# First block up to the solve: engines in a fixed order, key weights first, the norm factor inside the scaling, values later

## The chip, the core and the metric

The kernel runs on one core of a Trainium2 chip. The metric is the time of one execution in device microseconds (us). The core has TensorE (PE in the rows; its weight loads are PEld), VectorE (DVE), ScalarE (ACT), GpSimd (POOL) and SyncE (SP), which here only issues DMA transfers. Each engine has a queue of its own and works it off strictly in order; an instruction that waits holds up all that stands behind it on that engine.

## The reference

Two transformer blocks run one after the other on 256 tokens of width 1024, each ending in a mixture of experts. The change touches the start of the first block. There the tokens `x` and 256 context tokens `ctx` are normed and modulated with vectors that come from the conditioning input `c`:

```python
m_lat = jnp.split((s_lat @ w_mod[l] + b_mod[l])[:, None, :], 6, axis=-1)
h_lat = modulate(rmsnorm(x_lat, norm1_g[l]), m_lat[0], m_lat[1])
h_ctx = modulate(rmsnorm(x_ctx, norm1_g[l]), m_ctx[0], m_ctx[1])
mix_lat, mix_ctx = token_mixers(h_lat, h_ctx, w_in[l], ...)
```

`token_mixers` projects h with `w_in` into the inputs of four token mixers. One of them, the gated delta net, needs keys, values and queries (after a convolution of five taps and a SiLU), a decay `g` and a factor `beta`, and in every chunk the inverse of a triangular matrix:

```python
lower = jnp.where(strict, jnp.einsum('bnhid,bnhjd->bnhij', kb, kc) * decay, 0.0)
t_inv = lax.linalg.triangular_solve(eye + lower, eye, left_side=True, lower=True, unit_diagonal=True)
```

The matrix needs keys, decay and beta. Values and queries come in only when the inverse is there.

## The kernel before

All token data is kept with features on the partitions and 512 tokens (256 of `x`, 256 of `ctx`) in the free dimension. Every float32 product that matters is made of three: a weight is split into `whi` (a rounded copy, ScalarE) and `wlo` (the rest, a subtraction), the activations into `hh` and `hl`, and PE multiplies whi by hh, whi by hl and wlo by hh (`mm3`, L275). `wsplit` makes the pair for 128 output columns; a counter `nsplit` gives every `share`-th `wlo` to GpSimd and the others to VectorE.

`block1` runs in this order:

- norm: squares of x1 and xctx, their sums on PE (`san`, `ssn`), and `rs` by a logarithm and an exponential on ScalarE (L289, L290), for each half apart; x1 and xctx are multiplied by it in place (L638), and x1 is loaded again later (L658).
- `shift_scale(j)`, j from 0 to 7: loads 1 MB of `w_mod_a`, multiplies on PE (`ma`), copies (`msa`), folds on PE (`mq`), and makes shift `modT` and scale `A` of feature block j (L607, L608).
- the key loop, k from 0 to 7: `modulated(k)` makes `ht` (GpSimd, L618, for some k ScalarE), `hh` and `hl`; then come six products into the key sums `pk[0]`, `pk[1]` (`pj` in the rows) and two into `abp`, the inputs of decay and beta.
- behind it: convolution of both key halves (`conv`: a copy `raw` on ScalarE, five passes `cacc` on VectorE, a SiLU), the value projections, decay and beta, the norm of the keys (`l2`), outer products `rE` on GpSimd (L771), their sums `pE` and `brow` on PE, the key products `gram`, and from these `Lc` and its transpose `Lt` on VectorE.
- `solve()`: 31 steps on VectorE, each a product `tmp` (L837) and a sum `X` (L838), then two transposes `Y`.
- `projections()`, woven into the solve as filling: queries, gate, `nk`, `nq`, `nv`, `dv`, `dk`, `dq` and `fu`, each a weight load `win`, two splits and two times 24 products (L275) of 512 or 256 columns, and `mods`, which multiplies further parts of `w_mod` (`mp`). `totok` turns a projected value to token order by PE transposes (`tk`) and a copy by `S.evac`, which takes ScalarE and VectorE in turn.

Behind this come the mixers (`delta`, attention, Fourier), the output projection, the experts, and the second block.

What sets the order: a scheduler orders each engine's queue by the program's order and by when it takes an instruction to be ready. `keep_in_program_order` binds an instruction to its place in the program. Weights go through a ring of four slots of 1 MB that SyncE fills in program order; a load waits until its slot's last reader is done, and the loads behind it wait too.

Of the kernel before, what the change touches and what calls it, by code (L numbers as in the profile page):

```python
# [9 lines left out]
F32 = mybir.dt.float32  # L10
# [170 lines left out]

class K:
# [331 lines left out]
def block1(S):  # L514
# [43 lines left out]
    nc.scalar.activation(sc[:, :, 0:3], V("c3").rearrange("p (k i) -> p k i", i=3), AF.Silu)  # L558

# [36 lines left out]
    def shift_scale(j):  # L596
# [11 lines left out]
        nc.vector.scalar_tensor_tensor(A1[:, j, :], q[:, 2:4], bm1[:, j:j + 1], bc(V("g1")[:, j:j + 1], [128, 2]), op0=ALU.add, op1=ALU.mult)  # L608

    def modulated(k):  # L610
        for i, x in enumerate((x1, xctx)):
            t = he.tile([128, 256], F32, name="ht", bufs=3)
            q = slice(256 * i, 256 * i + 256)
            a, b = A1[:, k, i:i + 1], S.modT[:, k, i:i + 1]
            if i == 1 and k % 2:
                nc.scalar.activation(t, x[:, k, :], AF.Identity, bias=b, scale=a)
            else:
                nc.gpsimd.tensor_scalar(t, x[:, k, :], a, b, op0=ALU.mult, op1=ALU.add)  # L618
# [20 lines left out]
    for j in (1, 2):  # L639
        shift_scale(j)  # L640
# [1445 lines left out]
```

## Time and profile before

| | us |
|---|---|
| three runs | 2063.32, 2068.43, 2068.35 |
| median | 2068.35 |
| the profiled execution, time | 2067.2 |
| the profiled execution, span | 2065.4 |
| first key product (PE) | 26.66 |
| last product of the key loop (PE) | 57.28 |
| first product of the filling (PE) | 89.30 |
| last step of the solve ends (DVE) | 153.38 |
| last copy of the filling (ACT) | 202.97 |
| first load of the output projection's weights | 330.96 |

The page's first part gives PE 1651.5 us busy (80%), DVE 648.3 (31%), ACT 446.4 (22%) and POOL 207.9 (10%). The shares are means over stages with different limits: from about 350 to 1290 us the DMA engines are full with the experts' weights, while before that PE, the chains on ACT and DVE, and PE's granted clock matter. So the first 203 us are read stage by stage.

### The profile page before, as it was taken

The page shows a single profiled execution, that of the slowest core. Times are in us where ns is not written, and L with a number is a line of the kernel's source. Part 1 is how long each engine was busy: PE and PEld are TensorE (multiplying, and loading weights), DVE is VectorE, ACT ScalarE, POOL GpSimd, SP SyncE. Part 2 cuts the span into 40 slices and gives each one's busy share as a digit, 9 for nine tenths or more (in the row PEclk, how much of TensorE's full clock was granted, in tenths as well). Part 3 has the DMA queues.
Part 4 walks back from the last instruction along what each step waited for, and adds up shares of the span by engine and source line. Part 5 has one row for each costly group of instructions (what it writes and reads, how often), then busy time and mean ns, then how long its engine had stood idle before and what let it go on. Part 6 is the DMA issues. An engine that isn't in the chain of part 4 may idle for free.

```text
span 2065.4 us, 25484 instructions
## 1 busy us (share of the span) xinstructions
PE 1651.5 (80%) x10702; PEld 853.1 (41%) x10702; DVE 648.3 (31%) x1326; ACT 446.4 (22%) x794; POOL 207.9 (10%) x273
## 2 busy tenths in 40 slices
PE   6879999866666667566666666899998999999997
PEld 3656457511121112111121111788998444444443
DVE  4793683311111111001011110799655121222212
ACT  4542233300010001000010001576543111111111
POOL 2433432100000000000000000243111000000000
PEclk8999999888887887888898788999999999999998
DMA  7466457999999999999999999434548899999994
GB/s 296 144 218 228 159 203 314 416 431 430 431 431 430 431 430 430 431 431 431 430 431 431 430 430 427 162 124 153 203 182 337 353 431 430 430 430 431 431 430 195
DMA packets 61798, 723.70 MB, mean 350 GB/s; under 512 B 6944, under 2 KB 8736, under 8 KB 11120
## 3 DMA queue, kind: packets, MB, share of 16 engines
q1 hardware_dynamic: 60560, 717.95, 83.8%
q0 software_dynamic: 1120, 4.08, 0.5%
q8 instruction: 86, 1.41, 0.3%
q14 instruction: 32, 0.26, 0.0%
HBM read 720.96 MB, written 1.05 MB: 350 GB/s over the span
## 4 chain that ended last, share of the span: by engine, by line
DMA 47%; PE 38%; DVE 9%; ACT 3%; issue 2%; POOL 1%; SPq 0%; DVEq 0%; ACTq 0%; POOLq 0%
DMA w_up<-in_w_up_dram 15%; DMA w_down<-in_w_down_dram 14%; DMA w_gate<-in_w_gate_dram 13%; PE pj L275 6%; PE Yp L1852 5%; PE U L1852 4%; PE G L1852 4%; DMA w<-in_w_dram 4%; PE pw L275 2%; PE gx L1852 2%; DVE tmp L837 1%; PE ya L275 1%; PE cmb L1852 1%; PE mp L545 1%; PE yb L275 1%
## 5 line engine op out<-in xcount | busy, mean ns | idle before, releaser
L1221 PE MATMUL U<-w_up,xg 128*32 128x512 f32 x1024 | 172.8, 808 | 119.8 <-DMA w_up<-in_w_up_dram 119.8
L1221 PE MATMUL Yp<-w_down,hT 128*32 128x512 f32 x1024 | 161.5, 762 | 101.7 <-DMA w_down<-in_w_down_dram 96.2
L1221 PE MATMUL G<-w_gate,xg 128*32 128x512 f32 x1024 | 160.0, 676 | 57.8 <-DMA w_gate<-in_w_gate_dram 57.7
L1329 DVE TENSOR_TENSOR hs<-hs,U 128x512 f32<-128x512 f32 x16 | 11.0, 687 | 437.2 <-PE U L1221 437.2
L1221 PEld LDWEIGHTS U<-w_up,xg 128*32 128x32 f32 x1024 | 33.2, 129 | 259.8 <-DMA w_up<-in_w_up_dram 162.8
L275 PE MATMUL pj<-uh,whi 128*128 128x256 f32 x408 | 118.1, 290 | 3.2 <-ACT uh L1452 3.2
L1221 PEld LDWEIGHTS Yp<-w_down,hT 128*32 128x32 f32 x1024 | 31.5, 124 | 210.9 <-DMA w_down<-in_w_down_dram 140.0
L1852 PE MATMUL U<-w,xg 128*64 128x512 f32 x512 | 113.7, 594 | 6.0 <-DMA w<-in_w_dram 6.0
L275 PE MATMUL pj<-uh,wlo 128*128 128x256 f32 x408 | 116.7, 286 | 1.1 <-DVE wlo L257 1.1
L275 PE MATMUL pj<-ul,whi 128*128 128x256 f32 x408 | 115.7, 284 | 0.0
L1852 PE MATMUL Yp<-w,hT 128*64 128x512 f32 x512 | 113.8, 596 | 2.3 <-DVE ysl L1924 1.6
L1852 PE MATMUL G<-w,xg 128*64 128x512 f32 x512 | 112.6, 592 | 0.0
L1343 ACT COPY ys<-Yp 128x256 f32<-128x256 f32 x17 | 6.3, 373 | 479.0 <-DVE ys L1342 479.0
L256 ACT CAST whi<-win 128x1024 fp32r<-128x1024 f32 x72 | 75.1, 1048 | 71.4 <-PE pj L275 41.6
L1221 PEld LDWEIGHTS G<-w_gate,xg 128*32 128x32 f32 x1024 | 29.4, 115 | 145.0 <-DMA w_gate<-in_w_gate_dram 87.1
L1221 PE MATMUL cmb<-seln,ys 128*128 128x256 f32 x256 | 78.6, 422 | 13.0 <-DVE ys L1342 9.5
L1465 POOL DMA_DIRECT2D dist<-in_dist_dram x1 | 0.6, 606 | 877.0 <-DMA w_down<-in_w_down_dram 877.0
L1342 DVE COPY ys<-Yp 128x256 f32<-128x256 f32 x17 | 7.2, 424 | 244.9 <-PE Yp L1221 244.9
L1339 DVE SCALAR_TENSOR_TENSOR x<-cmb,modT,x 128x256 f32<-128x256 f32 x128 | 59.5, 483 | 77.0 <-PE cmb L1221 77.0
L275 PEld LDWEIGHTS pj<-uh,whi 128*128 128x128 f32 x408 | 77.5, 190 | 5.1 <-ACT uh L1452 3.4
L275 PEld LDWEIGHTS pj<-uh,wlo 128*128 128x128 f32 x408 | 77.5, 190 | 2.4 <-DVE wlo L257 1.5
L1221 PEld LDWEIGHTS cmb<-seln,ys 128*128 128x128 f32 x256 | 43.4, 195 | 83.3 <-DVE x L1339 37.3
(583 smaller groups left out, 2949.1 us busy)
## 6 DMA issues: line engine op xcount, KB each, us to landing
w<-in_w_dram SPq DMA_DIRECT2D x94, 2048.0 KB, 25.6
w_gate<-in_w_gate_dram SPq DMA_DIRECT2D x64, 2048.0 KB, 38.8
w_up<-in_w_up_dram SPq DMA_DIRECT2D x64, 2048.0 KB, 38.8
w_down<-in_w_down_dram SPq DMA_DIRECT2D x60, 2048.0 KB, 38.9
wmod<-in_w_mod_dram SPq DMA_DIRECT2D x40, 1024.0 KB, 4.9
win<-in_w_in_dram SPq DMA_DIRECT2D x36, 1024.0 KB, 4.9
wmod<-in_w_mod_a_dram SPq DMA_DIRECT2D x8, 1024.0 KB, 7.4
wout<-in_w_out_dram SPq DMA_DIRECT2D x8, 1024.0 KB, 6.9
```

What stands on the lines that cost most here:

```text
L256: self.nc.scalar.copy(hi, x)
L275: self.nc.tensor.matmul(out, a(k), b(k), start=(n == 0), stop=(n == 3 * K - 1))
L545: nc.tensor.matmul(out, l, r, start=a, stop=b)
L837: nc.vector.tensor_tensor(tv, X[:, 0:i, 0:i], bc(Lt[:, i, None, 0:i], [128, i, i]), op=ALU.mult)
L1221: nc.tensor.matmul(out, l, r, start=a, stop=b)
L1329: nc.vector.tensor_tensor(hs, hs, U, op=ALU.mult)
L1339: nc.vector.scalar_tensor_tensor(x1[:, k, :], pc, S.modT[:, 40 + k, 0:1], x1[:, k, :], op0=ALU.mult, op1=ALU.add)
L1342: nc.vector.tensor_copy(ys[:, 0:256], Y[:, 0:256])
L1343: nc.scalar.copy(ys[:, 256:512], Y[:, 256:512])
L1465: nc.gpsimd.dma_start(dist, I["dist"])
L1852: tc.keep_in_program_order(nc.tensor.matmul(o, l, r, start=a, stop=b))
```

## The change

- A wrapper `Engines` binds every TensorE, VectorE and ScalarE instruction from the key weights' load to the solve's input `Lt` to its place in the program. GpSimd and SyncE stay with the scheduler.
- The key weights `win` are loaded ahead of the eight `wmod` loads, and are split before the norm's logarithm.
- The norm factor: one logarithm and one exponential over both halves; `rs` enters the scaling (`ht` = x times A times rs on VectorE), ScalarE adds the shift for `hh`, VectorE makes `hl`. x1 and xctx are not written, and x1 is not loaded again.
- `shift_scale` has two halves that are placed between the key products of the step before.
- `warm` issues products whose result nobody reads: six ahead of the norm's sums and two behind each of the first two `ma`.
- The value projections and the turning of values and keys to token order move from before the solve into `projections()`.
- GpSimd loses `ht`, the outer products and, by `share` staying at 4 during the solve, most `wlo`; the copies `egl` move behind the solve's input. `totok` copies on ScalarE only.
- Behind the keys, ScalarE does exponentials first, then both SiLU and squares, both logarithms, both exponentials.

```diff
+class InOrder:
+    def __getattr__(self, name):
+        f = getattr(self.engine, name)
+        return lambda *a, **k: self.tc.keep_in_program_order(f(*a, **k))
+class Engines:
+    def __init__(self, tc):
+        self.tensor, self.vector, self.scalar = (InOrder(tc, e) for e in (tc.nc.tensor, tc.nc.vector, tc.nc.scalar))
+        self.gpsimd, self.sync = tc.nc.gpsimd, tc.nc.sync
...
+    def warm(self, pool, tag, n):
+        p = pool.tile([128, 512], F32, name="warm", tag=tag)
+        for _ in range(n):
+            self.tc.keep_in_program_order(self.tc.nc.tensor.matmul(p[:, 0:256], self.c("ones"), self.C[:, 0:256], start=True, stop=True))
...
+            nc.vector.scalar_tensor_tensor(t[:, q], x[:, k, :], A1[:, k, i:i + 1], rs[:, q], op0=ALU.mult, op1=ALU.mult)
+            nc.scalar.activation(H[0][:, k, q], t[:, q], AF.Identity, bias=S.modT[:, k, i:i + 1])
+            nc.vector.scalar_tensor_tensor(H[1][:, k, q], t[:, q], S.modT[:, k, i:i + 1], H[0][:, k, q].bitcast(F32), op0=ALU.add, op1=ALU.subtract)
...
+    nc = S.nc = Engines(tc)
+    wk = wload(0)
+    blocks = [shift_scale(j) for j in range(8)]
...
     for k in range(8):
-        if k < 5:
-            shift_scale(k + 3)
-        if k == 5:
-            wv = wload(1)
-            wvs = [S.wsplit(sb, wv, 0, tags=("Lc", "Lt"))]
-        modulated(k)
+        if k < 6:
+            next(blocks[k + 2])
+        keys(0, k)
+        if k < 7:
+            modulated(k + 1)
+        if k < 6:
+            next(blocks[k + 2])
+        keys(1, k)
...
-    wvs.append(S.wsplit(sp, wv, 1))
-    nc.gpsimd.dma_start(x1, I["xl"].rearrange("p (k t) -> p k t", k=8))
+    wv = wload(1)
+    wvs = S.wsplit(sb, wv, 0, tags=("Lc", "Lt"))
...
-        S.evac(dst[:, :, 128 * P:128 * P + 128], tp)
+        S.evac(dst[:, :, 128 * P:128 * P + 128], tp, "s")
...
-        nc.gpsimd.tensor_tensor(dst, bc(vec[:, None, :], [128, 32, vec.shape[1]]), bc(mask[:, :, None], [128, 32, vec.shape[1]]), op=ALU.mult)
+        nc.vector.tensor_tensor(dst, bc(vec[:, None, :], [128, 32, vec.shape[1]]), bc(mask[:, :, None], [128, 32, vec.shape[1]]), op=ALU.mult)
...
     def projections():
+        for P in range(2):
+            a = conv(proj(wv, P, 512, None if P else wvs), 4 + P, 512)
+            yield 5.1
+            totok(vtok, a, P)
+        for P in range(2):
+            totok(ktok, kn[:, P, :], P)
...
-    S.share = 1
     weave(solve(), fill)
```

SyncE now issues the key weights `win` behind x1 and xctx, then the small `wab` and all eight `wmod`; before, one `wmod` stood ahead of the key weights and seven behind.

ScalarE at the norm of the keys, before: `l2rk` is the norm factor of a half, by a logarithm (L289) and an exponential (L290), `eg` and `D` are exponentials for the decay.

```order
L289 ACTIVATE l2rk_561<-l2p,cst 128x512
L290 ACT_TABLE_LOAD
L290 ACTIVATE l2rk_561<-l2rk_561 128x512
L761 ACTIVATE eg<-gp 128x192
L289 ACT_TABLE_LOAD
L289 ACTIVATE l2rk_569<-l2p,cst 128x512
L290 ACT_TABLE_LOAD
L290 ACTIVATE l2rk_569<-l2rk_569 128x512
L782 ACTIVATE D<-pE 128x512 x2
```

And after, from the SiLU of the keys (`cacc`) on (in this listing every ordered instruction carries the wrapper's line, L189; `l2k` is a square, `ln` the decay's logarithm):

```order
L189 ACT_TABLE_LOAD
L189 ACTIVATE cacc<-cacc 128x512
L189 ACTIVATE l2k<-cacc 128x512
L189 ACTIVATE cacc<-cacc 128x512
L189 ACTIVATE l2k<-cacc 128x512
L189 ACT_TABLE_LOAD
L189 ACTIVATE ln<-u_481 128x32
L189 ACTIVATE l2rk<-l2p,cst 128x512 x2
L189 ACT_TABLE_LOAD
L189 ACTIVATE l2rk<-l2rk 128x512 x2
```

From the keys' SiLU to the last exponential of the key norm there are three table loads now; before, there were six (the ones at L681, L731 and L733 stand ahead of the rows shown).

VectorE at the solve's start, before (L678 and L680 are convolution passes of the queries; `t` and `Lc` build the solve's input, `Lt` is its transpose):

```order
L824 TENSOR_TENSOR Lc<-t_740,beta 128x32x16
L825 TENSOR_TENSOR t_740<-D,gm 128x512
L826 TENSOR_TENSOR Lc<-t_740,brow 128x32x16
L678 TENSOR_SCALAR cacc<-raw,vec_97 128x256
L828 STREAM_TRANSPOSE Lt<-Lc 128x32x32
L250 COPY ktok<-tk 128x4x128
L837 TENSOR_TENSOR tmp<-X,Lt 128x1
```

And after:

```order
L189 TENSOR_TENSOR Lc<-t_626,beta 128x32x16
L189 TENSOR_TENSOR t_626<-D,gm 128x512
L730 TENSOR_SCALAR cacc<-raw,vec_97 128x512
L189 TENSOR_TENSOR Lc<-t_626,brow 128x32x16
L732 SCALAR_TENSOR_TENSOR cacc<-raw,vec_97,cacc 128x512
L189 STREAM_TRANSPOSE Lt<-Lc 128x32x32
L732 SCALAR_TENSOR_TENSOR cacc<-raw,vec_97,cacc 128x512
L895 TENSOR_TENSOR tmp<-X,Lt 128x1
```

The first pass over the first value half (L730) now stands ahead of the last `Lc`.

VectorE at the solve's end, before, where `nv` is a copy by `totok` and `Y` the solve's result:

```order
L837 TENSOR_TENSOR tmp<-X,Lt 128x900
L838 TENSOR_REDUCE X<-tmp 128x30
L837 TENSOR_TENSOR tmp<-X,Lt 128x961
L838 TENSOR_REDUCE X<-tmp 128x31
L250 COPY nv<-tk 128x4x128
L842 STREAM_TRANSPOSE Y_1299<-X 128x1024
```

And after, where L274 makes the `wlo` of the two `nv` halves:

```order
L895 TENSOR_TENSOR tmp<-X,Lt 128x841
L274 TENSOR_TENSOR wlo<-win,whi 128x1024
L896 TENSOR_REDUCE X<-tmp 128x29
L274 TENSOR_TENSOR wlo<-win,whi 128x1024
L895 TENSOR_TENSOR tmp<-X,Lt 128x900
L896 TENSOR_REDUCE X<-tmp 128x30
```

The copy has left VectorE's queue, and two splits for PE's filling stand behind the product of step 29.

## Rows read from the trace of the kernel before

**Rows 1.** Busy time by stretch: us, PE, PEld, DVE, ACT, POOL, granted clock, DMA share, GB/s.
```profile
600.00:1200.00 600.00, 388.98 (x2232) 101.27 (x2236) 58.55 (x118) 30.45 (x71) 0.00 (x0) 0.81 1.01 431
```

**Rows 2.** Timeline of SP's DMA issues: start us, us, what, count.
```profile
330.96 5.53 SPq L238 DMA_DIRECT2D wout<-in_w_out_dram  x4
```

**Rows 3.** Timeline at the start: start us, us, engine, line, what [idle before, releaser].
```profile
11.67 1.06 ACT L433 ACTIVATE sqn<-xctx 128x1024 f32<-128x1024 f32 x1 [1.40 <-DMA xctx<-in_xctx_dram]
...
19.52 0.40 PE L282 MATMUL ma<-wmod,sc 128*32 128x256 f32 x1 [0.40 <-DMA wmod<-in_w_mod_a_dram]
...
21.35 1.98 ACT L256 CAST whi<-win 128x1024 fp32r<-128x1024 f32 x2
...
26.66 0.76 PE L545 MATMUL pj<-hh,whi 128*128 128x512 f32 x1 [6.07 <-DVE hh L620]
```

**Rows 4.** Busy time by stretch, columns as in Rows 1: the clock's falls and rises.
```profile
24.00:26.00 2.00, 0.00 (x0) 0.00 (x0) 2.00 (x2) 0.09 (x1) 2.00 (x1) 0.50 0.00 0
36.00:38.00 2.00, 2.00 (x19) 0.98 (x19) 0.36 (x1) 0.24 (x1) 0.00 (x0) 0.70 0.01 4
150.00:152.00 2.00, 0.00 (x0) 0.00 (x0) 1.97 (x2) 0.00 (x0) 0.00 (x0) 0.50 0.00 0
164.00:166.00 2.00, 2.00 (x13) 1.36 (x15) 0.00 (x0) 0.00 (x0) 0.00 (x0) 1.00 0.00 0
```

**Rows 5.** Timeline of PE inside the key loop, columns as in Rows 3.
```profile
40.48 0.40 PE L282 MATMUL ma<-wmod,sc 128*32 128x256 f32 x1
...
41.48 0.45 PE L545 MATMUL abp<-hh,wabs 128*64 128x512 f32 x1
...
42.23 0.50 PE L545 MATMUL mq<-cst,msa 128*128 128x2 f32 x4
...
42.59 0.48 PE L545 MATMUL pj<-hl,whi 128*128 128x512 f32 x1
```

**Rows 6.** Timeline from the key loop's end to the first filling projection.
```profile
57.73 0.58 ACT L675 COPY raw<-pj 128x512 f32<-128x512 f32 x1
...
57.92 2.39 POOL L257 TENSOR_TENSOR wlo<-win,whi 128x1024 fp32r<-128x1024 f32 x1 [1.50 <-ACT whi L256]
...
58.34 2.25 DVE L678 TENSOR_SCALAR cacc<-raw,vec 128x512 f32<-128x512 f32 x1 [0.42 <-ACT raw L675]
...
63.75 4.05 DVE L680 SCALAR_TENSOR_TENSOR cacc<-raw,vec,cacc 128x512 f32<-128x512 f32 x6
...
76.10 1.28 ACT L290 ACT_TABLE_LOAD   x1
...
86.07 2.07 PE L545 MATMUL brow<-rE,cst 128*128 128x512 f32 x2
...
88.08 1.30 PE L545 MATMUL gram<-kn 64*32 64x32 f32 x112
...
89.30 0.38 PE L275 MATMUL pj<-hh,whi 128*128 128x256 f32 x1
```

**Rows 7.** Timeline of the work beside and behind the solve.
```profile
154.11 1.09 PE L703 MATMUL tk<-cst,vfm 128*128 128x128 f32 x4 [9.26 <-DVE nv L250]
...
158.13 0.80 PE L275 MATMUL pj<-hh,wlo 128*128 128x512 f32 x1 [2.08 <-DVE wlo L257]
...
175.37 0.48 PE L275 MATMUL pj<-hh,whi 128*128 128x512 f32 x1
...
181.16 0.62 PE L282 MATMUL mp<-wmod,sc 128*32 128x512 f32 x1
...
202.97 0.37 ACT L252 COPY fu<-pj 128x256 f32<-128x256 f32 x1 [2.40 <-PE pj L275]
```

**Rows 8.** Groups by line, 0 to 210 us: xcount | busy us, mean ns | idle before.
```profile
L837 DVE TENSOR_TENSOR tmp<-X,Lt 128x1 f32<-128x1 f32 (+30 forms) x31 | 29.9, 964 | 0.8
...
L257 DVE TENSOR_TENSOR wlo<-win,whi 128x1024 fp32r<-128x1024 f32 x9 | 12.0, 1342 | 10.2 <-ACT whi L256 10.2
...
L838 DVE TENSOR_REDUCE X<-tmp 128x1 f32<-128x1 f32 (+30 forms) x31 | 15.6, 502 | 0.8
```

More of the change, by code (lines that the diff above doesn't have):

```diff
@@ L608, in shift_scale @@
         nc.vector.scalar_tensor_tensor(A1[:, j, :], q[:, 2:4], bm1[:, j:j + 1], bc(V("g1")[:, j:j + 1], [128, 2]), op0=ALU.add, op1=ALU.mult)
+        yield
     def modulated(k):
+        t = sb.tile([128, 512], F32, name="ht", tag="cacc", bufs=2)
         for i, x in enumerate((x1, xctx)):
-            t = he.tile([128, 256], F32, name="ht", bufs=3)
             q = slice(256 * i, 256 * i + 256)
[L614 to L618, printed above, removed]
@@ new lines, in modulated @@
+        for i in range(2):
+            q = slice(256 * i, 256 * i + 256)
+            nc.vector.scalar_tensor_tensor(H[1][:, k, q], t[:, q], S.modT[:, k, i:i + 1], H[0][:, k, q].bitcast(F32), op0=ALU.add, op1=ALU.subtract)
+    nc = S.nc = Engines(tc)
+    wk = wload(0)
+    blocks = [shift_scale(j) for j in range(8)]
+    sqs = []
+    for x in (x1, xctx):
+        sq = [sp.tile([128, 4, 256], F32, name="sqn", tag=t) for t in ("whi", "wlo")]
+        nc.scalar.activation(sq[0], x[:, 0:4], AF.Square)
+        nc.vector.tensor_tensor(sq[1], x[:, 4:8], x[:, 4:8], op=ALU.mult)
+        sqs.append(sq)
@@ new lines, in block1 @@
+    san, ssn = (ps.tile([128, 512], F32, name=n, tag="mm") for n in ("san", "ssn"))
+    stn = sb.tile([128, 512], F32, name="stn", tag="T2b")
+    rs = sb.tile([128, 512], F32, name="rs1", tag="T2", bufs=2)
+    S.warm(ps, "mm", 6)
+    for i, sq in enumerate(sqs):
+        q = slice(256 * i, 256 * i + 256)
+        for k in range(8):
+            j = k % 4
+            mm(san[32 * j:32 * j + 32, q], S.c("ones")[:, 0:32], sq[k // 4][:, j, :], k < 4, k >= 4)
+        nc.vector.tensor_copy(stn[:, q], san[:, q])
@@ L634, in block1 @@
+    for i in range(2):
+        q = slice(256 * i, 256 * i + 256)
+        mm(ssn[:, q], bc(S.c("sel32")[:, 0:1], [128, 128]), stn[:, q])
+    wks = [S.wsplit(sp, wk, P) for P in range(2)]
+    S.rsqrt(rs, ssn, 1.0 / 1024)
+    nc.sync.dma_start(wab, I["w_ab"].rearrange("p (k f) -> p k f", k=8))
+    next(blocks[0])
+    S.warm(ps, "mm", 2)
+    next(blocks[0])
+    next(blocks[1])
+    S.warm(ps, "mm", 2)
+    modulated(0)
+    next(blocks[1])
     wabs = he.tile([128, 8, 64], F32R, name="wabs")
@@ L674, in conv, with conved @@
         nc.gpsimd.memset(raw[:, :, 258:260], 0.0)
-        nc.scalar.copy(raw[:, :ns, 2:258], p.rearrange("p (s t) -> p s t", t=256))
+        nc.scalar.copy(raw[:, :n // 256, 2:258], p.rearrange("p (s t) -> p s t", t=256))
+        return raw
+    def conved(raw, cidx, n):
+        ns = n // 256
         acc = sb.tile([128, 512], F32, name="cacc", tag="cacc", bufs=2)
@@ L715, in block1 @@
         mm(abt[:, 16 * t:16 * t + 16], abT[0:64, 128 * t:128 * t + 128], C("sel32")[0:64, 0:16])
+    ka = [conved(raws[0], 2, 512)]
     ab = sm.tile([128, 4, 16], F32, name="ab")
@@ L828, in block1 @@
     nc.vector.transpose(Lt.rearrange("p i j -> p j i"), Lc)
+    nc = S.nc = tc.nc
+    egl = sm.tile([128, 4, 2, 4, 2], F32, name="egl")
+    for e in range(2):
+        for s in range(4):
+            nc.gpsimd.tensor_copy(egl[64 * e:64 * e + 64, s], egl_all.rearrange("p s d t (q e) -> p s d t q e", e=2)[64 * e:64 * e + 64, s, :, :, :, e])
     X = sb.tile([128, 32, 32], F32, name="X", tag="Xl")
```

112 lines of the change are left out of this document (51 added, 61 removed).

## The prediction

> **What bounds the kernel now.** I first read the stretch table of the middle. From 600 to 1200 us the DMA engines' share is 1.01 while PE is busy 389 of 600 us [rows 1], so there the weights of the experts set the pace. Then I read SyncE's timeline for where that stream begins: at 330.96 us the first weights of the output projection are issued [rows 2], and none of them depends on the first 203 us except by their place in the queue. If the mixers end earlier, the stream begins earlier by as much and everything behind it moves along. So I take a microsecond saved before 202.97 us (the last copy of the filling) as one saved at the end; the sum is about that stretch alone. The profiled execution took 2067.2 us, 1.15 below the median of 2068.35, and a difference from it is carried to the median unchanged.
>
> In the timeline of the first 203 us I looked for when PE does not work and for when it works at half clock. PE waits 6.07 us for the first `hh` and starts the key products at 26.66 [rows 3]. The granted clock is 0.50, the lower level of 1.2 GHz, at 24 to 26 us, and the mean of 0.70 from 36 to 38 puts its rise to 2.4 GHz near 37.2; it is low again at 150 to 152 and back at 164 to 166 [rows 4]. Both falls come after PE has stood nearly idle. Between the key loop's end and the filling's start (57.7 to 89.30) the chain is one of ScalarE, VectorE and PE in turns [rows 6]. Behind the solve PE waits 9.26 us for a copy of `nv` that stands in VectorE's queue behind the last steps, then 2.08 us for a `wlo` [rows 7].
>
> **The change part by part.** *Start.* Between xctx's landing (11.67) and the second `wmod`'s (19.52) lie 3.13 MB (two `wmod`, the key weights, the small `wab`), so 2.5 us for each MB [rows 3]. In the new order the key weights land at 14.2, `wmod` blocks at 17.0, 19.5 and 22.0. ScalarE splits the key weights from 14.2 in 2 us, the length of the two casts now [rows 3]; then the logarithm and the exponential with a table load of 1.28 each [rows 6] give `rs` near 20.1. The copy of the first `ma`, its fold, shift and scale follow by 21.4, and PE does a `ma` group (1.0 us, 40.48 to 41.48), four `warm` and a `mq` (0.36) [rows 5] that stand ahead of the first key product: 24.8. The `warm` products cost nothing here, as PE has no other work. Gain 1.9 us.
>
> *Key loop.* 64 products of 512 columns remain behind this point. A projection of 24 of them takes 5.8 us at full clock (175.37 to 181.16) [rows 7], 0.24 each, so 15 us; with six `ma` groups (6.0) and six `mq` (2.2) [rows 5] the last product ends near 47.9. Before, it began at 26.66 and ended at 57.3, the start of the next link being 57.73 [rows 6]: 31 us for about the same work, of which 10.5 ran at half clock (26.66 to 37.2) and lost some 5.3 us. I take full clock, because PE now has `ma` and `warm` products through the wait. If the clock is low once more, it is 53. Gain at this point 9.8, the start's 1.9 among them.
>
> *From the keys to the filling.* Before this took from 57.7 to 89.3, 31.6 us. Now, step by step with durations of rows 6: the first key half is summed at 46.7, but the split of the second value half stands ahead on ScalarE (1 us, half of the two casts of rows 3), so `raw` ends at 48.4. That split's `wlo` still goes to GpSimd, as the counter's fourth, and holds VectorE's first pass as it does now: `cacc` took 2.25 us beside a `wlo` of 2.39, where a pass takes 0.675 in the group of six. First convolution 53.4, second 57.1 with small decay operations between. A SiLU and a square at `raw`'s 0.58 each: 58.3. A table load 59.6, the decay's logarithm, two logarithms, a load (62.5), two exponentials 63.8; the scaling of both key halves 64.5. The outer products, now on VectorE at 0.7 each, are done by 62.7 and are off this path; three table loads remain between SiLU and the end instead of six. Then `gram` 1.7 and `brow`, which took 2.07 at the low clock and so about 1.1 at the high one, with the other sums: 67.5. That is at full clock. But the value projections, which filled PE here before, are gone from the gap, and PE has next to nothing between 52 and 57 us. In the trace both stretches in which PE stood nearly idle were followed by some 13 us at the low clock [rows 4]. So I add 4 us for `gram`, the sums and the first filling at half speed, and take 71.5 for the filling's start. Without the fall it is 67.5; with the key loop low as well it is 76.
>
> The Trainium skill, TensorE: Matmul & The Clock Gate, section "Why this matters for your kernels", says that gaps between bursts of matmuls return TensorE to its lower clock, and by that rule the change takes from the gap the very work that kept the clock up. The trace agrees as far as it goes (0.50 behind both idle stretches); by the rule the filling starts at 71.5, and by the row before the change alone, where the gap was filled, at 67.5.
>
> *Filling and solve.* Before, the filling ran from 89.3 to 202.97, 113.7 us. Added: two value projections, 2 times 5.8 = 11.6, and 2 us as the first starts at low clock. Removed: one group of `mp`, 1.0; the 9.26 for `nv`, because `totok` copies on ScalarE only and the copy no longer stands behind the last solve steps; the 2.08 for a `wlo`; and the low clock that followed the wait, 154 to 163 us, 4.3 [rows 4, 7]. New: most `wlo` are now VectorE's (by counting the splits, 17 of 22 before the end of the filling instead of 9, at 1.34 us each [rows 8]), and the two of `nv` stand behind the `tmp` of step 29. The solve's 31 steps take 29.9 + 15.6 us [rows 8] plus what stands between. VectorE reaches that place about 60.6 us behind the filling's start and PE wants it at 56.7: a new wait of 3.9. Also VectorE's first pass over the first value half stands ahead of the last `Lc`, so the solve waits for one projection more; it still starts near 77 to 81 instead of 99, and is not last. Sum: 113.7 + 11.6 + 2 - 1.0 - 9.3 - 2.1 - 4.3 + 4 = 114.6. The filling ends at 71.5 + 114.6 = 186.1 instead of 203.0, a gain of 17.
>
> The Trainium skill, SBUF — State Buffer, section "Who interferes with whom", states that VectorE and GpSimd lock a shared port pair against each other, so that one blocks while the other runs. The trace shows it in the 2.25 us of `cacc` [rows 6]; by that rule the loss of GpSimd's work is a gain except for the one split left at just that place.
>
> What is undone at no cost: x1 is not loaded again (1 MB, hidden behind other work); `egl` is off the path. The new order of ScalarE puts the splits of later weights where PE still has products.
>
> **The rivals.** *The clock holds.* PE keeps the high level through the chain, since the gap is short, or the first filling work restores it at once: 4 us and the 2 us of the first projection are saved, 2051 - 6 = 2045. For it: the first key half's `abp` and folds lie near the gap. Against it: both falls in rows 4.
>
> *The clock falls twice.* The wait of 3.9 for `nv`'s splits is followed by a low stretch, like the 9.26 before: up to 4.3 lost again, and 2 to 4 us if the key chain has a wait that I don't see: 2051 + 4 to 8, so 2055 to 2059.
>
> *The gain is not carried.* Loads go in program order through four slots, and an earlier filling wants the same loads sooner; if a load waits for a slot that the late `nv` splits hold, or the mixers behind wait for a transfer, most of the gain goes at 202.97: about 2064, inside 0.3%. Against it: at 163 us and later PE has no wait for a load in the rows.
>
> *VectorE sets the pace, slower.* Eight splits stand between `brow` and the solve's end on VectorE (queries, gate, `nk`, `nq`, `nv`). Should each hold PE for the 3.9 us that I find for `nv` alone, it is 31 instead of 4, so 27 more: 2078. The point from which this is slower than before by 0.3%: (17 + 6.2 + 4) / 8 = 3.4 us for each split. Against it: a split takes 1.34, and before the solve's steps grow VectorE reaches the splits soon, as a step takes (29.9 + 15.6) / 31 = 1.5 us in the mean [rows 8].
>
> **How the numbers follow.** 0.3%, about what a measurement of this kernel can tell, is 6.2 us: faster is below 2062.1, slower above 2074.6. The forecast, 2068.35 - 17 = 2051, has 0.45 and its own range of 2046 to 2057; the clock holds, 0.16; it falls twice, 0.14; not carried, 0.14; VectorE paces, 0.11. Faster is 0.45 + 0.16 + 0.14 = 0.75, same 0.14, slower 0.11. The range goes from 2040 (the 2045 with as much again on sizes) to 2066 (the not carried case), and leaves out the slower case and some of the edges.
>
> **What would show it.** First key product near 25 and last near 48 with the clock at 1.00 from 27 on, or the key loop is wrong. `kn` near 64 and the filling's first product at 67 to 72, with a clock of 0.50 at 60 to 70 if the forecast is right, and 1.00 if the first rival is. No wait of PE near the solve's end over 4 us; its last copy near 186. The output projection's first load, 330.96 before, should come 17 us earlier; if it does not, the gain was not carried. A `wlo` of VectorE that PE waits for more than twice in the solve points to the slower case. Wrong above all would be the sum if PE's idle time in the solve is not where I put it: the wait for `nv` is the largest single term, 9.3 of 17.

## The result, and the profile after

| | before | after |
|---|---|---|
| median of five runs, us | 2067.38 | 2056.02 |
| lowest and highest, us | 2063.32, 2068.43 | 2052.55, 2059.58 |
| the profiled execution: time, span, us | 2067.2, 2065.4 | 2052.55, 2050.8 |
| first and last product of the key loop (PE), us | 26.66, 57.28 | 24.76, 48.16 |
| first product of the filling (PE), us | 89.30 | 71.22 |
| the solve's first step to the start of its last transpose (DVE), us | 99.16 to 155.77 | 82.79 to 139.56 |
| last copy of the filling (ACT), us | 202.97 | 186.44 |
| first issue of the experts' `w_up` (SP), us | 350.10 | 335.22 |

The ratio is 0.9948, with a 95% interval of 0.9935 to 0.9961: the change saves 11 us, between 8 and 13. 2051 was forecast, and 2056 lies in the range.

PE's timeline of the changed kernel (start us, us, engine, line, what, idle before and who ended it; every ordered instruction carries the line L189):

```profile
24.76 0.50 PE L189 MATMUL pj<-hh,whi 128*128 128x512 f32 x1
...
48.16 0.40 PE L189 MATMUL abp<-hl,wabs 128*64 128x512 f32 x1
...
57.91 2.08 PE L189 MATMUL l2p<-l2k,bd 128*128 128x512 f32 x2 [5.74 <-ACT l2k L189]
...
61.78 1.75 PE L189 MATMUL l2p<-l2k,bd 128*128 128x512 f32 x2
...
67.93 1.12 PE L189 MATMUL pE<-rE,cst 128*128 128x512 f32 x2 [2.42 <-ACT eg L189]
...
71.22 0.80 PE L292 MATMUL pj<-hh,whi 128*128 128x512 f32 x1
...
131.03 0.55 PE L292 MATMUL pj<-hh,wlo 128*128 128x512 f32 x1 [4.42 <-DVE wlo L274]
```

These rows answer to [rows 3, 6 and 7]. The first key product has lost its wait of 6.07. The second `l2p` starts 3.9 us behind the first, and the filling's one wait near the solve's end is now 4.42 us, for a `wlo`, where 9.26 for `nv` and 2.08 for a `wlo` stood. The clock by stretch, columns as in [rows 1], answers to [rows 4]:

```profile
26.00:28.00 2.00, 2.00 (x22) 1.07 (x21) 1.78 (x6) 0.13 (x1) 0.00 (x0) 1.00 1.00 414
...
55.00:60.00 5.00, 2.09 (x6) 0.59 (x10) 3.27 (x6) 4.32 (x9) 0.13 (x2) 0.62 0.95 400
60.00:65.00 5.00, 5.00 (x22) 2.25 (x22) 3.19 (x14) 3.24 (x5) 0.00 (x0) 0.69 0.39 115
65.00:70.00 5.00, 2.58 (x120) 1.32 (x121) 2.54 (x5) 3.95 (x7) 1.21 (x8) 1.00 0.24 98
...
130.00:140.00 10.00, 8.97 (x34) 7.18 (x35) 9.86 (x9) 1.20 (x3) 0.00 (x0) 0.83 0.61 233
```

The key loop runs at 1.00 (the row of 26 to 28 us stands for all of them up to 48). The clock falls once behind the keys (0.62, then 0.69) and once behind the wait at 131 (0.83).

Behind the filling, the timelines of ScalarE, GpSimd, VectorE and PE:

```profile
186.44 0.37 ACT L269 COPY fu<-pj 128x256 f32<-128x256 f32 x1 [3.84 <-PE pj L292]
...
189.26 0.90 POOL L1148 DMA_DIRECT2D nab<-in_na_bias_dram  x1 [1.60 <-issue]
...
196.34 0.43 DVE L1151 TENSOR_TENSOR ns<-ns,nab 128x256 f32<-128x256 f32 x1 [7.17 <-DMA nab<-in_na_bias_dram]
...
198.15 1.03 PE L568 MATMUL pa<-S,wT 128*32 128x128 f32 x4 [4.33 <-DVE S L1075]
```

`nab` is a bias for the neighbour attention, loaded in two parts of 512 KB. GpSimd issues the first 2.8 us behind the last copy; VectorE waits 7.17 us for it, with the copies of the state `S` behind it in its queue, and PE waits 4.33 for `S`. Before, the load was issued 0.6 us behind the last copy and VectorE waited 3.34:

```profile
203.57 0.78 POOL L1085 DMA_DIRECT2D nab<-in_na_bias_dram  x1
...
210.89 0.43 DVE L1088 TENSOR_TENSOR ns<-ns,nab 128x256 f32<-128x256 f32 x1 [3.34 <-DMA nab<-in_na_bias_dram]
```

SyncE's issues in the changed kernel, then in the kernel before:

```profile
311.48 9.10 SPq L255 DMA_DIRECT2D wout<-in_w_out_dram  x4
...
335.22 0.33 SPq L255 DMA_DIRECT2D w_up<-in_w_up_dram  x1
```

```profile
350.10 0.33 SPq L238 DMA_DIRECT2D w_up<-in_w_up_dram  x1
```

The weights that [rows 2] shows at 330.96 are issued 19.5 us earlier, but the first `w_up` only 14.9. From there to the end both take the same: 2050.8 - 335.22 = 1715.6 and 2065.4 - 350.10 = 1715.3.

So the trace saves 16.5 us at the last copy of the filling, 14.9 at `w_up` and 14.65 in the time of the profiled executions. The medians show 11.4: the profiled execution of the changed kernel is the fastest of its five, 3.5 below their median, that of before stands 0.2 from its median. Of the 16.5 us, 1.9 come at the first key product, 7.2 in the key loop and 9.0 from there to the filling's start; the filling itself takes 1.5 us longer (115.2 instead of 113.7), with two value projections more in it.

### The profile page after: what moved, and what is told of

Its sections match the earlier page's. It is cut to its first block, busy times and chain, and to the rows that moved or that the text cites. A ratio compares the mean times of both kernels' runs of the same rounds, so it can differ in the third digit from the quotient of the medians.

```text
span 2050.8 us, 25504 instructions
## 1 busy us (share of the span) xinstructions
PE 1648.2 (80%) x10722; PEld 855.3 (42%) x10722; DVE 634.9 (31%) x1338; ACT 440.4 (21%) x795; POOL 169.5 (8%) x248
## 4 chain that ended last, share of the span: by engine, by line
DMA 47%; PE 39%; DVE 7%; ACT 3%; issue 2%; POOL 1%; SPq 0%; DVEq 0%; ACTq 0%; POOLq 0%
DMA w_up<-in_w_up_dram 15%; DMA w_down<-in_w_down_dram 14%; DMA w_gate<-in_w_gate_dram 13%; PE pj L292 7%; PE Yp L1915 5%; PE U L1915 4%; PE G L1915 4%; DMA w<-in_w_dram 4%; PE pw L292 2%; PE gx L1915 2%; PE ya L292 1%; PE mp L568 1%; PE cmb L1915 1%; PE yb L292 1%; DVE wlo L274 1%
## 5 line engine op out<-in xcount | busy, mean ns | idle before, releaser
L1915 PE MATMUL U<-w,xg 128*64 128x512 f32 x512 | 113.7, 594 | 6.3 <-DMA w<-in_w_dram 6.3
L1284 PEld LDWEIGHTS G<-w_gate,xg 128*32 128x32 f32 x1024 | 29.5, 115 | 149.0 <-DMA w_gate<-in_w_gate_dram 91.3
L274 DVE TENSOR_TENSOR wlo<-win,whi 128x1024 fp32r<-128x1024 f32 x54 | 66.9, 1241 | 35.3 <-ACT whi L273 35.2
L292 PEld LDWEIGHTS pj<-ul,whi 128*128 128x128 f32 x408 | 77.6, 190 | 0.5 <-issue 0.3
## 6 DMA issues: line engine op xcount, KB each, us to landing
w<-in_w_dram SPq DMA_DIRECT2D x94, 2048.0 KB, 25.8
```

The source lines that it names most:

```text
L274: (lo_eng or self.nc.vector).tensor_tensor(lo, x, hi.bitcast(F32), op=ALU.subtract)
L292: self.nc.tensor.matmul(out, a(k), b(k), start=(n == 0), stop=(n == 3 * K - 1))
L1284: nc.tensor.matmul(out, l, r, start=a, stop=b)
L1915: tc.keep_in_program_order(nc.tensor.matmul(o, l, r, start=a, stop=b))
```

## The experiments

All medians, in us; every ratio is against runs of the kernel before that were made beside it on the same chip (their medians lie between 2067.4 and 2067.9). "Fill" is the first product of the filling, "fu" its last copy, `w_up` its first issue, all from the profiled execution. In p2 three products of the filling stand ahead of the one that is listed, the first at 80.6.

| run | median | ratio, 95% interval | first key | fill | fu | w_up |
|---|---|---|---|---|---|---|
| the change | 2056.0 | 0.9948, 0.9935 to 0.9961 | 24.8 | 71.2 | 186.4 | 335.2 |
| a1_no_warm | 2058.0 | 0.9954, 0.9941 to 0.9967 | 24.8 | 72.8 | 189.5 | 338.8 |
| a2_totok_turns | 2050.3 | 0.9927, 0.9912 to 0.9941 | 24.2 | 69.8 | 184.8 | 329.1 |
| a3_share_one | 2065.0 | 0.9993, 0.9982 to 1.0004 | 25.8 | 73.0 | 202.1 | 351.1 |
| a4_outer_pool | 2051.6 | 0.9928, 0.9913 to 0.9942 | 24.9 | 72.0 | 188.1 | 334.4 |
| b1_v0_gap | 2046.9 | 0.9906, 0.9890 to 0.9921 | 26.3 | 71.4 | 180.4 | 326.9 |
| b2_nv_pool | 2054.0 | 0.9929, 0.9916 to 0.9943 | 26.8 | 76.0 | 190.5 | 337.3 |
| c1_warm_gap | 2057.2 | 0.9942, 0.9928 to 0.9955 | 24.2 | 71.2 | 188.0 | 342.2 |
| d1_nab_sp | 2048.1 | 0.9901, 0.9886 to 0.9916 | 24.5 | 70.1 | 186.5 | 328.7 |
| f1_gap_nab | 2041.5 | 0.9876, 0.9861 to 0.9892 | 24.9 | 70.4 | 181.3 | 323.6 |
| f2_gap_nab_turns | 2043.2 | 0.9881, 0.9865 to 0.9896 | 24.8 | 71.9 | 182.0 | 326.7 |
| p1_before_totok (on before) | 2066.3 | 0.9994, 0.9985 to 1.0003 | 27.0 | 87.1 | 198.6 | 344.5 |
| p2_before_warm (on before) | 2061.0 | 0.9972, 0.9961 to 0.9983 | 34.1 | 86.5 | 196.5 | 341.7 |

From `w_up` to the end every profiled execution took 1715.2 to 1719.1 us, so what an edit does is done by `w_up`, to within 4 us. A mark is that of one execution, and the five of the change spread over 7 us: where marks and medians differ, the medians count.

**The copies of `totok`, the largest term of the sum.** On the kernel before, the edit alone:

```diff
-        S.evac(dst[:, :, 128 * P:128 * P + 128], tp)
+        S.evac(dst[:, :, 128 * P:128 * P + 128], tp, "s")
```

> The kernel before with one edit, the copies of totok on ScalarE only. Theory (the prediction's largest term): the wait of 9.26 us for nv at 154 goes, with the 2.08 behind it and the low clock: the last fu copy moves from 203.0 to 188 to 192, the end is 11 to 15 us earlier than before. Rival: the split of dv stands on VectorE behind the same last steps and both transposes, so PE waits for that instead, until about 158: the last fu copy within 3 us of 203, the end within 3 us of before.

Measured 0.9994, no change to be told. PE's timeline has one wait near the solve's end:

```profile
154.28 0.80 PE L275 MATMUL pj<-hh,wlo 128*128 128x512 f32 x1 [7.24 <-DVE wlo L257]
```

The 9.26 for `nv` is gone and 7.24 for the next `wlo` stands at the same place: VectorE makes it behind the last steps and both transposes. A wait of 3.69 us for the queries' squares, at 106.69, is new. The last copy came 4.4 us earlier, 2.2 of which were there at the filling's start. The rival holds for the wait and for the end; for the last copy it had said 3 us at most. The reverse edit, on the changed kernel:

```diff
-        S.evac(dst[:, :, 128 * P:128 * P + 128], tp, "s")
+        S.evac(dst[:, :, 128 * P:128 * P + 128], tp)
```

> The changed kernel with the copies of totok on ScalarE and VectorE in turn again, as before the change. Theory (the prediction's largest term): the nv copy stands behind the last solve steps again and PE waits some 9 us for it, with a low clock behind it: the last fu copy moves from 186.4 to 196 to 200, the end is 9 to 13 us later. Rival: in the new order the solve ends at 141 us with PE still busy, the copy is not what PE needs next, and the two nv splits move one step earlier: the last fu copy within 2 us of 186.4, the end unchanged.

The last copy is at 184.8, as the rival has it, but the end is 6 us earlier, which neither theory expected. GpSimd's and VectorE's rows behind the filling:

```profile
186.00 0.90 POOL L1148 DMA_DIRECT2D nab<-in_na_bias_dram  x1
...
191.34 0.43 DVE L1151 TENSOR_TENSOR ns<-ns,nab 128x256 f32<-128x256 f32 x1 [3.80 <-DMA nab<-in_na_bias_dram]
```

The load of `nab` is issued 3.3 us sooner, half of which is the earlier last copy, and VectorE waits 3.80 instead of 7.17. Whether the copies or the load gave the 6 us is the question of f2 below.

**Who makes `wlo` during the solve.**

```diff
+    S.share = 1
     weave(solve(), fill)
     S.share = 4
```

> The changed kernel with all wlo of the solve's time on GpSimd again. Theory (the prediction's): VectorE loses its splits, but GpSimd's reads hold tmp products of the solve for up to 2 us each; the wait for nv's wlo goes and one for a later wlo or for the solve comes: the last fu copy within 3 us of 186.4, the end within 3 us. Rival: VectorE's splits are what PE waits for, the solve ends sooner without them: the last fu copy 4 to 6 us earlier.

Both missed. The time goes back to that of the kernel before (0.9993), 9 us behind the change, and the filling takes 129.1 us instead of 115.2. (The marks lie 16 us apart at `w_up`, because the profiled execution here was 3.8 above its median and that of the change 3.5 below.) VectorE's groups between 60 and 205 us (xcount | busy us, mean ns | idle before), of the change and then of this run:

```profile
L274 DVE TENSOR_TENSOR wlo<-win,whi 128x1024 fp32r<-128x1024 f32 x14 | 17.9, 1279 | 21.9 <-ACT whi L273 21.8
L895 DVE TENSOR_TENSOR tmp<-X,Lt 128x1 f32<-128x1 f32 (+30 forms) x31 | 17.0, 550 | 0.4
L896 DVE TENSOR_REDUCE X<-tmp 128x1 f32<-128x1 f32 (+30 forms) x31 | 15.5, 501 | 0.5
```

```profile
L895 DVE TENSOR_TENSOR tmp<-X,Lt 128x1 f32<-128x1 f32 (+30 forms) x31 | 23.7, 764 | 0.7
L896 DVE TENSOR_REDUCE X<-tmp 128x1 f32<-128x1 f32 (+30 forms) x31 | 15.5, 501 | 0.6
...
L274 DVE TENSOR_TENSOR wlo<-win,whi 128x1024 fp32r<-128x1024 f32 x8 | 10.6, 1322 | 28.8 <-ACT whi L273 28.7
L730 DVE TENSOR_SCALAR cacc<-raw,vec 128x512 f32<-128x512 f32 (+1 forms) x4 | 5.6, 1393 | 2.1 <-ACT raw L722 2.1
```

The products `tmp` take 23.7 us instead of 17.0 while ten `wlo` run on GpSimd instead of four; the sums `X` take 15.5 in both. The first passes of the four convolutions (L730) take 5.6 us instead of 1.7. PE's waits in this run:

```profile
95.34 1.11 PE L760 MATMUL tk<-cst,cacc 128*128 128x128 f32 x4 [4.80 <-ACT cacc L738]
...
110.28 0.87 PE L568 MATMUL l2p<-l2q,bd 128*128 128x256 f32 x2 [2.22 <-ACT l2q L749]
...
145.44 0.79 PE L292 MATMUL pj<-hh,wlo 128*128 128x512 f32 x1 [6.99 <-DVE wlo L274]
```

The first two hang on convolutions on VectorE, the third on a `wlo` behind a solve whose last transpose starts 7.6 us later than in the change (1.8 of it at the solve's start). The Trainium skill, SBUF — State Buffer, section "Who interferes with whom", says that a VectorE product of two operands in SBUF contends with GpSimd's reads and that a reduction does not. The trace agrees: 17.0 against 23.7, 15.5 against 15.5.

**The warm products and the clock of the key loop.** On the changed kernel:

```diff
-    S.warm(ps, "mm", 6)
...
-    S.warm(ps, "mm", 2)
...
-    S.warm(ps, "mm", 2)
```

> The changed kernel without its ten warm products; everything else as it is. The warm products write a result that nobody reads, so nothing of the computation is left out. Theory (the prediction's): they hold TensorE's granted clock at 1.00 through the norm and the first wmod blocks; without them PE has about 6 us less work before 24.8 us and the key loop begins at 0.50, as it did before the change: the last key product moves from 48.2 to about 53 us, the filling's start from 71.2 to about 76, the end 5 us later. Rival: the eight wmod products that now stand between the key products are dense enough by themselves; the clock stays at 1.00 from 26 us on, and the marks move by less than 1 us (a little earlier, since the products ahead of the first mq are gone).

The loop's last product moved by 0.5 us, the filling's start by 1.6, the last copy by 3.0 and the end by 2.0, which is within the intervals. The clock by stretch of this run, and of a3, which has the warm products:

```profile
22.00:24.00 2.00, 1.77 (x16) 1.25 (x20) 1.49 (x6) 1.28 (x4) 0.00 (x0) 0.64 1.01 410
24.00:26.00 2.00, 2.00 (x11) 1.04 (x4) 1.11 (x4) 1.04 (x3) 0.00 (x0) 0.51 1.03 430
26.00:28.00 2.00, 2.00 (x14) 1.32 (x17) 1.88 (x6) 0.14 (x1) 0.00 (x0) 1.00 0.99 410
```

```profile
22.00:24.00 2.00, 2.00 (x8) 1.65 (x7) 1.07 (x3) 1.35 (x4) 0.00 (x0) 0.50 1.02 426
24.00:26.00 2.00, 2.00 (x19) 1.06 (x20) 1.47 (x5) 0.04 (x1) 0.00 (x0) 0.66 0.98 406
26.00:28.00 2.00, 2.00 (x12) 1.52 (x11) 1.18 (x5) 1.14 (x3) 0.00 (x0) 1.00 0.97 393
```

Either way it was low for some 3 or 4 us at about 24 and back at 1.00 by 26. The rival holds for the key loop: with `ma` products and key products without a gap the clock came up again and stayed. Its marks behind the loop moved by more than the 1 us that it allowed; there the clock was 0.66 from 70 to 75 us, where the change has 1.00. On the kernel before, where the gap is 6 us:

```diff
-    for j in (1, 2):
-        shift_scale(j)
+    shift_scale(1)
+    S.warm(ps, "mm", 10)
+    shift_scale(2)
```

> The kernel before with one edit, ten warm products (5.6 us of PE) between the first two wmod groups and the key loop. They write a result that nobody reads. Theory: the clock stays at 1.00 up to the first key product, the 10.5 us at half clock (26.66 to 37.2) are gone, the key loop's last product moves from 57.3 to about 52, the end 5 us earlier. Rival: the loop was paced by ScalarE, VectorE and GpSimd making hh and hl, so with a full clock PE only waits more: last product at 56 to 57, end within 1 us.

The median fell by 6.4 us, as the theory had it, but not where it had it:

```profile
34.08 0.50 PE L551 MATMUL pj<-hh,whi 128*128 128x512 f32 x1
...
150.85 1.09 PE L710 MATMUL tk<-cst,vfm 128*128 128x128 f32 x4 [7.17 <-DVE nv L250]
```

The clock did not stay up: behind a wait of 3.95 us for `msa` it was 0.50 from 26 to 28 us, and it was back at 1.00 from 30, ahead of the first key product. The warm products and what was queued behind them held that product back by 7.4 us. The loop then took 21.8 us instead of 30.6, so its last product came only 1.4 earlier. The rest came later, 1.4 up to the filling's start and 3.7 in the filling, where the wait for `nv` was 7.17 without a second one behind it (and a new one of 1.86 stood at 120.8, for a `wlo` of GpSimd).

**The gap behind the keys.** Work in it that nobody reads:

```diff
+    S.warm(ps, "mm", 10)
     ka = [conved(raws[0], 2, 512)]
```

> The changed kernel with ten more warm products (5.6 us, their result is not read) in the gap of 5.74 us between the keys' inputs of decay and the first l2p. It changes the clock there alone. Theory: the granted clock stays at 1.00 from 55 to 65 us (0.62 and 0.69 now), the two l2p take 1.1 instead of 2.08 and 1.75, the filling starts 2 to 4 us earlier than 71.2, and the end follows by as much. Rival: the chain is ScalarE's (two table loads, logarithms, exponentials), PE's speed there is hidden: the filling starts within 1 us of 71.2.

The filling starts at 71.2, as the rival has it, though for another reason:

```profile
55.00:60.00 5.00, 3.77 (x24) 0.88 (x16) 2.68 (x5) 4.33 (x6) 0.13 (x2) 1.00 0.75 249
60.00:65.00 5.00, 3.15 (x14) 1.49 (x12) 4.17 (x16) 4.96 (x8) 0.00 (x0) 0.93 0.93 369
65.00:70.00 5.00, 4.54 (x132) 2.88 (x133) 3.00 (x7) 1.49 (x4) 1.21 (x8) 0.50 0.06 18
```

The clock is 1.00 where it was 0.62, the keys are scaled at 65.2 instead of 67.5, but then the clock is 0.50 from 65 to 70, where it was 1.00, and the sums take the gain back. The Trainium skill, TensorE: Matmul & The Clock Gate, section "Why this matters for your kernels", says that gaps between bursts lower the clock; the trace agrees in the gap and leaves open why the level fell behind it, where PE had waited 1.68 us. The median is 1.2 above the change, within the intervals. With work that is needed:

```diff
+    pv = proj(wv, 0, 512, wvs)
     ka = [conved(raws[0], 2, 512)]
...
-            a = conv(proj(wv, P, 512, None if P else wvs), 4 + P, 512)
+            a = conv(proj(wv, P, 512) if P else pv, 4 + P, 512)
```

> The changed kernel with the first value projection (24 products, 5.8 us) put back ahead of the solve, into the 5.74 us in which PE waits for the squares of the keys. Theory (the prediction's sum, in which PE's work adds up): the clock stays high through the chain and the filling has 5.8 us less to do: the last fu copy moves from 186.4 to about 179, the end 7 us earlier. Rival (the solve is the bound in the middle of the filling): VectorE makes the nv splits when the solve lets it, at about 130 us, so PE, 6 to 8 us earlier there, waits 10 to 12 us instead of 4.4, the last fu copy within 2 us of 186.4, the end unchanged; the value convolution on VectorE ahead of the last Lc can even make it later.

From the first key product to the last copy it took 154.1 us instead of 161.7, so 7.5 less, where the prediction had put 5.8 and 2 for this projection: 1.3 of it up to the filling's start, 6.2 in the filling. The clock was 1.00 from 55 to 75 us. The median is 9.1 below the change. The wait for `nv`'s split did not grow:

```profile
123.85 0.79 PE L292 MATMUL pj<-hh,wlo 128*128 128x512 f32 x1 [5.02 <-DVE wlo L274]
```

since the solve came earlier too (78.9 instead of 82.8). In the change VectorE's first `Lc` waited for the first value projection to end:

```profile
77.21 0.69 DVE L189 TENSOR_TENSOR Lc<-t,beta 128x512 f32<-128x512 f32 x1 [4.83 <-PE pj L292]
```

`Lc` doesn't read that projection, but the split of its weights lies in the buffers that `Lc` and `Lt` take (`tags=("Lc", "Lt")`), so PE has to be done with it first. With the projection ahead, this wait is gone. The additive theory holds.

**The split that PE waits for.**

```diff
-                S.evac(t, proj(w, P, 512), "s")
+                S.evac(t, proj(w, P, 512, lo_eng=tc.nc.gpsimd if i == 6 else None), "s")
```

(`lo_eng` is handed through to the engine of `wlo`.)

> The changed kernel with the two wlo of nv on GpSimd. Theory (additive): the wait of 4.42 at 131 and the low clock behind it go, 6 us: the last fu copy at about 180. Rival (the solve is the bound): PE is released at nv, and stands next for the wlo of dv, which VectorE makes only behind both Y, near 141 to 142: a wait of 2 to 4 us there, the last fu copy at 183 to 186, the end 0 to 3 us earlier.

```profile
147.99 0.79 PE L292 MATMUL pj<-hh,wlo 128*128 128x512 f32 x1 [3.82 <-DVE wlo L274]
```

The wait went to the `wlo` of `dv`, as the rival has it; the end is 2.0 below the change, within the intervals. The last copy, 190.5, is later than either said; 2.0 of that was there at the first key product.

**The load of `nab`.**

```diff
-                nc.gpsimd.dma_start(bias[P], I["na_bias"].rearrange("p (c h k) -> p c h k", c=2, h=4)[:, :, 2 * P:2 * P + 2, :])
+                nc.sync.dma_start(bias[P], I["na_bias"].rearrange("p (c h k) -> p c h k", c=2, h=4)[:, :, 2 * P:2 * P + 2, :])
```

> The changed kernel with one line changed behind the filling: the two loads of nab (the neighbour bias, 512 KB each) go through SyncE's queue instead of GpSimd's. Theory: in the changed kernel GpSimd issues the first of them 2.8 us behind the last fu copy, VectorE waits 7.2 us for it with the copies of S behind it, PE waits 4.33 for S, and its clock falls; this is where the gain that the profile had at 186 us was not carried. With the load issued at 186 to 187 PE's wait falls below 1.5 us, wout is issued 4 to 6 us earlier than 311.5, the end 4 to 6 us earlier. Rival: the transfer takes as long on either queue, since the chi, tim and wmod loads share the DMA engines: wout within 1.5 us of 311.5.

```profile
190.77 0.43 DVE L1151 TENSOR_TENSOR ns<-ns,nab 128x256 f32<-128x256 f32 x1 [1.58 <-DMA nab<-in_na_bias_dram]
...
328.69 0.33 SPq L255 DMA_DIRECT2D w_up<-in_w_up_dram  x1
```

VectorE's wait is 1.58 instead of 7.17, and PE's wait for `S` is gone. `w_up` comes 6.5 us earlier with the last copy at the same place, and the median is 7.9 below the change. `wout` moved by 1.0 only, so that mark of the expectation missed; what held its first load stays open. The theory holds for the end. Over all runs, the stretch from the last copy to `w_up` took 142.2 to 144.7 us in the three kernels with `nab` on SyncE, 148.8 to 154.3 in the three in which GpSimd issued it late (the change, a1, c1), and 144.3 to 149.0 in the other eight, with a3 at the upper end.

**Both edits.**

> The changed kernel with two edits together: the first value projection back in the gap ahead of the solve, and the nab loads through SyncE's queue. Theory: the two gains lie in different stretches (about 7.5 us ahead of the last fu copy, about 6 behind it) and add up: last fu copy near 180, w_up first issued near 322 instead of 335, the end 12 to 15 us earlier than the changed kernel's 2056, so 2041 to 2044. Rival: with the filling shorter, GpSimd and SyncE come to the nab loads sooner in any case (one edit alone already had a wait of 3.7 for nab instead of 7.2), so the second edit adds 2 to 4 us at most: 2044 to 2046.

```profile
181.26 0.37 ACT L269 COPY fu<-pj 128x256 f32<-128x256 f32 x1 [3.86 <-PE pj L292]
...
323.61 14.06 SPq L255 DMA_DIRECT2D w_up<-in_w_up_dram  x3
```

2041.5, 14.5 below the change and 26 below the kernel before: the gains, 9.1 and 7.9 alone, add up but for 2.5, and this kernel is the fastest of all.

> The same two edits, and the copies of totok on ScalarE and VectorE in turn again. Theory: the 6 us which that edit alone gave came from the nab load being issued sooner, not from the copies, so nothing is left of it here: the end within 2 us of the kernel with two edits. Rival: the copies on ScalarE delay its splits and squares in the filling and cost 2 to 4 us: the end earlier by that.

2043.2, not faster than without the edit, so the copies give nothing here. That what a2 gained came with the load of `nab` is the likely reading and not shown: no run has a2's copies with the late load, and f2 differs from a2 in the gap too.

**The outer products.**

```diff
-        nc.vector.tensor_tensor(dst, bc(vec[:, None, :], [128, 32, vec.shape[1]]), bc(mask[:, :, None], [128, 32, vec.shape[1]]), op=ALU.mult)
+        nc.gpsimd.tensor_tensor(dst, bc(vec[:, None, :], [128, 32, vec.shape[1]]), bc(mask[:, :, None], [128, 32, vec.shape[1]]), op=ALU.mult)
```

> The changed kernel with the outer products rE on GpSimd again. Theory: they lie on the path from g to the sums pE; on GpSimd they take longer and, held against VectorE's gsub and kn, come later by 2 to 4 us: the filling starts at 73 to 76 instead of 71.2, and the end is later by as much. Rival: the path goes through the logarithms and exponentials of the key norm and the sums have slack: the filling within 1 us of 71.2 by its start, the end unchanged.

VectorE's and GpSimd's rows of this run, and `gsub` in the change:

```profile
62.86 2.35 DVE L189 TENSOR_SCALAR gsub<-g,cst 128x32 f32<-128x32 f32 x4
...
62.81 2.06 POOL L829 TENSOR_TENSOR rE<-g,cst 128x512 f32<-128x512 f32 x2 [4.07 <-DVE g L189]
```

```profile
62.78 0.68 DVE L189 TENSOR_SCALAR gsub<-g,cst 128x32 f32<-128x32 f32 x4
```

`gsub` is held (2.35 against 0.68), but the filling starts only 0.7 us later, counted from the first key product: the rival holds for the filling. The end is 4.4 us earlier than that of the change with the last copy 1.7 us later, so that gain isn't the outer products'. In this run GpSimd issued `nab` at once and VectorE waited 3.81.

## Why the prediction was right, and where it was not

**Start and key loop: right.** 24.8 and 47.9 were forecast; the first product started at 24.76, the last at 48.16. The loop ran at full clock as taken. The reason given, the warm products among the `ma`, was half wrong: without the warm ones the loop ended 0.5 us later (a1). That a high clock shortens the loop fits p2: with the clock at 1.00 the old loop took 21.8 us instead of 30.6, though some of its `wmod` products stood ahead of it there.

**From the keys to the filling: right sum, wrong parts.** 71.5 was forecast and 71.22 measured. Scaling ended at 67.5 instead of 64.5: the second convolution ended at 58.4 instead of 57.1, and the second logarithm waited 1.7 us for its `l2p`, ahead of which two groups of `mp` stood at half clock. In return the clock was back by 65, so that most of the 4 us allowed for a low clock up to the filling were not spent there. Two errors of about 3 us cancelled, and that was luck.

**Filling: right sum, wrong cause of the largest term.** 186.1 was forecast and 186.44 measured; the new wait at `nv`'s split was put at 3.9 and is 4.42; the value projections were put at 5.8 and 2 for the first, and b1 gives 7.5. But the 9.3 were put down to the copies of `totok`, and p1 and a2 show that the copies are worth nothing alone: the next `wlo` waits for the same end of the solve. The waits went with two other edits. With VectorE making its own splits and GpSimd quiet, `tmp` takes 17.0 us instead of 29.9 [rows 8], and with that undone (a3) 9 of the 11 us are gone. The prediction counted this edit as a cost, 17 splits on VectorE, and left `tmp` at its old 29.9. But the solve as a whole is no shorter, 56.8 us from its first step to its last transpose instead of 56.6: the splits and the value convolutions took up what `tmp` gave back, and PE has 11.6 us more to do meanwhile, the two value projections, where it waited 11.3 before. a3 shows that without the change of `share` the waits come back; that it would take them away by itself isn't shown, since no run has it on the kernel before. The solve started at 82.8, where 77 to 81 was forecast, and the projection that it waits for holds it by its buffer and not by the convolution pass (b1).

**The rival that ended slower was the wrong way round.** It held that VectorE's splits pace PE. In the whole filling PE waits over 1 us for one of them twice (4.42 and 1.09). They cost 1.28 us each, and with six more of them on GpSimd the solve takes 62.6 us instead of 56.8 (a3).

**The rival with two falls of the clock came true in its condition.** The clock fell behind the keys and again behind the wait at 131, and 2056 lies in its 2055 to 2059. But the second fall was short: 0.83 over 130 to 140 us, an estimated 1.7 us, and the last copy came within 0.4 us of the forecast. So this isn't where the gain was lost.

**Carried one to one: the step that failed.** From `w_up` on it holds to 0.3 us. Between the last copy and `w_up` it did not: 16.5 became 14.9. The sum took nothing for the stretch behind the filling; that the mixers wait there for a transfer stands in the prediction only as a part of the rival that isn't carried, with most of the gain lost. Here the load of `nab` was issued 2.8 us behind the last copy instead of 0.6, and VectorE waited 7.17 for it. d1 shows what a load through SyncE is worth there, 6.5 us at `w_up`, more than the 1.6 that was lost. The remaining 3.3 us between 14.65 and 11.4 are the place of the two profiled executions among their runs; the prediction carried the difference of one execution to the median.

**The range.** 2046 to 2057 for the forecast's own case holds the result; a gain of 11.4 is two thirds of the 17. The forecast started from 2068.35, the median of three runs; that of five is 1.0 lower.

**What stays open.** In the change, in a1 and in c1 GpSimd stood 1.6 us ahead of the issue of `nab`, with nothing in the profile that it waited for, and VectorE's wait was 7.2 to 8.4; in a2, a3, a4, b1 and b2, with the same instructions around it, it did not, and the wait was 3.7 to 4.1. With one profile of each, whether this belongs to the kernel or to the execution isn't settled; that the change showed it in the fastest of its five executions speaks for the kernel. Only a way around it was shown. And no run undoes the fixed order of the engines, the key weights' place, the norm factor inside the scaling or the three table loads: what each of them gives of the 18 us up to the filling's start is read from the traces, and their shares aren't shown.

## What to carry to other kernels

A wait that disappears from a queue is worth only the distance to the next instruction that waits for the same thing: look for that one before the wait is counted as a gain. An engine that is given more work can come out no slower when the engine that held up its products falls silent (`tmp`: 17.0 against 29.9), so the duration of its other instructions has to be re-estimated too. And the stretch right behind the one that is changed belongs to the sum: read which load or engine its first instruction waits for, and what issues that.

## What the runs showed of the hardware

The same opening instructions met different clocks. In the change the granted clock was 1.00 from 8 to 55 us; in b2 it was, by stretch

```profile
16.00:20.00 4.00, 3.08 (x19) 1.48 (x19) 1.82 (x2) 3.94 (x5) 0.00 (x0) 0.50 1.01 424
20.00:22.00 2.00, 2.00 (x11) 1.63 (x14) 0.13 (x1) 0.57 (x2) 0.00 (x0) 0.50 0.99 385
...
24.00:26.00 2.00, 2.00 (x13) 1.60 (x15) 1.01 (x3) 1.23 (x4) 0.00 (x0) 0.71 1.01 410
...
28.00:32.00 4.00, 4.00 (x32) 2.59 (x32) 2.52 (x8) 1.31 (x4) 0.00 (x0) 1.00 0.88 320
```

and the first key product came at 26.76 instead of 24.76. In all nine other kernels with the same opening it was low for a while between 8 and 26 us, in most of them around 14, and the first key product came between 24.15 and 26.76. The six warm products that end near 9 us did not prevent that; without them (a1) it was 1.00 from 8 to 22 us and low from 22 to 26. From 28 to 40 us the clock was 1.00 in all of them.

The low level in a chain moved rather than went: with the gap filled, it came some 8 us later (c1). With the value projection in the gap it was 0.70 and 0.53 from 65 to 70 us in f1 and f2, but 1.00 up to 75 in b1, so how a gap is filled doesn't settle it. And the two loads of `nab`, 512 KB each, took 6.0 to 8.4 us from issue to landing (median of the two) through GpSimd's queue, in the eleven kernels that issue them there, and 4.5 to 4.8 through SyncE's in d1, f1 and f2.
